# A long convolution at half-odd frequencies, over even and odd tokens, with its tables split in DRAM

## The chip, the cores and the metric

The kernel runs on one core of one Trainium2 chip. The metric is the device time of that core in microseconds, the median of several runs.

## The reference

The network has two blocks of two layers each, on 512 tokens of 1024 features. The change lies in the second block, in the long convolution of each layer (256 channels), whose kernel `k` is itself computed from the weights:

```python
    h_fwd = filt[:, :HY_WIDTH] * window
    h_bwd = filt[:, HY_WIDTH:] * window
    k = jnp.concatenate([h_fwd, jnp.zeros((1, HY_WIDTH), f32), h_bwd[:0:-1]], axis=0)
    return k * lax.rsqrt(jnp.sum(jnp.square(k), axis=0, keepdims=True) + 1e-6)
...
    k = hyena_filters(L, fw1, fb1, freq1, fw2, fb2, freq2, fw3)
    vf = jnp.fft.rfft(v, n=2 * L, axis=1)
    kf = jnp.fft.rfft(k, axis=0)
    y = jnp.fft.irfft(vf * kf[None], n=2 * L, axis=1)[:, :L]
    y = y + v * bias_d.astype(jnp.float32)
    return (y * x0.astype(jnp.float32)).astype(u.dtype)
```

With L = 512 this is a linear convolution of 512 tokens with taps at -511 to 511, by a transform of length 1024.

## The kernel before

**Products.** Every large product runs in three parts, so that it keeps the accuracy of float32: both factors are split into a high and a low part of type float32r, and `mm3` (line 347) issues high x high, high x low and low x high for each block of 128 rows. Weights come by a DMA from the SP queue into a staging buffer (`stage`, line 273); `split` (line 293) takes the high part on ACT (line 299) and the low part on DVE (line 300) into a pair of buffers of 1024 columns each, `hi` and `lo`. `pair` (line 278) hands out the pairs in turn: 3 are always there, and `more` adds some for a stretch; there are 6 in the feed-forward block of layer 1, and 3 in the part of the second block that holds the convolution. The buffers of a pair are free again when PE has read them for the last time. Staging buffers go round in the same way, 2 of them in the convolution. PSUM has 2 buffers `ps` of 512 columns that all products share, beside those that a stage opens for itself.

**Order.** Dependences and semaphores are set by the Tile framework from the order of the program. It also sets the order of the instructions on each engine: an instruction whose inputs and buffers are there earlier can stand ahead of one that comes earlier in the program. In the queue of an engine that order is then fixed, and an instruction that waits holds up what stands behind it. Streams that run beside the main one (`side`) give their steps at fixed amounts of work of the main stream.

**Spectra.** `spectrum` (line 1717) computes the transform of `k` for both layers of the second block. It runs as a side stream of the feed-forward block of layer 1, whose products are the main stream. After the filter network and the window (`sd`, sum and difference of both halves of the taps, split), it loads the table `fwd` in four parts of 256 columns (`ft`, a buffer of its own, one buffer), splits each, and multiplies: real parts with the sums, imaginary parts with the differences (two blocks of 128 frequencies in each part, 4 blocks of 128 tokens, 3 matmuls each). DVE multiplies the result with the norm `r` on its way to `K` (line 1790). A further product of 8 matmuls (line 1797) gives the highest frequency, which is packed in place of the imaginary part of frequency 0. `K` goes to DRAM (line 1801) and is loaded again by each layer's `Front` (line 1820).

**Convolution.** `second` (line 1903) runs, in the order of the program: the projections for the pooling (2 panels of 24 matmuls with 512 columns), the projections for the gate `x0` (2 such panels), beside them `values_t` (line 1858: the input of the convolution transposed, so that tokens lie on the partitions), then `transform` (line 1939), `token_values(0)` (line 1928: the first half of the attention's values, 4 blocks of tokens, 24 matmuls of 256 columns each) and `inverse` (line 1959). `attention` follows with the projections of its first head (lines 2051 to 2053).

`transform` has four blocks of 128 frequencies. For each, PE computes the real and the imaginary part in one `ps` buffer (2 x 12 matmuls of 256 columns); DVE multiplies with `K` (line 1953), POOL subtracts (line 1954), DVE adds (line 1955), and ACT and DVE split the product into `Y` (lines 360 and 361). `inverse` multiplies `Y` with the table `invt` into two `ps` buffers, one for each 128 channels (48 matmuls of 512 columns, lines 1968 to 1970); DVE, POOL, ACT and DVE finish (lines 1973 to 1975). For the tables, `transform` stages and splits four parts of `fwd`, `inverse` four parts of `invt`.

Of the kernel before, what the change touches and what calls it, by code (L numbers as in the profile page):

```python
# [18 lines left out]
S = 512  # L19
# [9 lines left out]
# ---------------------------------------------------------------------------  # L29
# host side: layout of the small vectors, tables that depend on shapes alone  # L30
# ---------------------------------------------------------------------------
# [63 lines left out]
def _constants():  # L95
# [22 lines left out]
    # attention rope: head_dim 64 = [r1 16 | r2 16 | c1 16 | c2 16], two heads on the partitions  # L118
# [12 lines left out]
    # window mask, keys [previous block | own | next]  # L131
# [4 lines left out]
    # retention rope: 64 row frequencies | 64 column frequencies  # L136
# [4 lines left out]
    # retention decay exponents  # L141
# [7 lines left out]
    # partial rope of the second block  # L149
# [11 lines left out]
    # pooling counts  # L161
# [6 lines left out]
    # hyena: position features, decay window, transform tables  # L168
# [7 lines left out]
    put("z", z)  # L176
# [4 lines left out]
    put("winf", win.reshape(4, 128, 256).transpose(1, 0, 2))  # L181
    put("winb", winb.reshape(4, 128, 256).transpose(1, 0, 2))
    con = np.ascontiguousarray(np.concatenate(out, axis=1))
    # forward [n, (cos f 0..511 | -sin f 0..511, with the Nyquist column in place of f=0)]
    fr = np.arange(512)
    ph = (2 * np.pi / 1024) * ((t[:, None].astype(np.int64) * fr[None]) % 1024)
    fwd = np.concatenate([np.cos(ph), -np.sin(ph)], axis=1)
    fwd[:, 512] = np.where(t % 2 == 0, 1.0, -1.0)
    invt = np.concatenate([2 * np.cos(ph.T), -2 * np.sin(ph.T)], axis=0) / 1024
    invt[0] = 1.0 / 1024  # L190
    invt[512] = np.where(t % 2 == 0, 1.0, -1.0) / 1024
    fwd = np.ascontiguousarray(fwd.astype(f).reshape(4, 128, 1024).transpose(1, 0, 2))
    invt = np.ascontiguousarray(invt.astype(f).reshape(8, 128, 512).transpose(1, 0, 2))
# [21 lines left out]
# ---------------------------------------------------------------------------  # L215
# device side
# ---------------------------------------------------------------------------
class Net:
# [22 lines left out]
    # -- small tables -------------------------------------------------------  # L241
# [14 lines left out]
    # -- weights ------------------------------------------------------------  # L256
# [8 lines left out]
    def stage_tile(self, some=slice(None)):  # L265
        """some: which of the rings"""
        rings = self.st_rings[some]
        n = self.si.setdefault(str(some), 0)
        pool, m = self.turn(rings, n)
        self.si[str(some)] += 1  # L270
        return pool.tile([128, 2048], F32, name=self.nm("st"), tag="st", bufs=m)
# [12 lines left out]
    def more(self, pairs, stages=0):  # L284
        """further buffers for weights"""
# [7 lines left out]
    def split(self, v):  # L293
        """f32 [128, k, c] -> hi, lo (f32r), exactly v = hi + lo up to float32's last bit"""
# [8 lines left out]
    # -- streams beside the main one, by the time of the tensor engine -------  # L303
# [13 lines left out]
    def side(self, gen, steady=False):  # L317
        """a generator whose steps each take so long; steady: on the whole, else each of them at least"""
# [12 lines left out]
    def cpanel(self, src, k, c, some=slice(None)):  # L331
        """[128, k, c] from DRAM, as pieces of 128 columns"""
# [3 lines left out]
    def kpanel(self, src, k, c):  # L336
        """[128, k, c] from DRAM, as pieces [128, 1, c]... of at most 1024 elements, listed by k"""
# [9 lines left out]
    # -- products -----------------------------------------------------------  # L347
# [15 lines left out]
    def rsqrt(self, pool, v, n):  # L363
        """[128, n] small: 1 / sqrt(v)"""
# [4 lines left out]
        # a first guess from the exponent and three steps of Newton's  # L369
# [1347 lines left out]
def spectrum(net, i, pool):  # L1717
# [61 lines left out]
    for n in range(2):  # L1779
        for j in range(2):  # L1780
# [4 lines left out]
            for jj in range(2):  # L1785
# [5 lines left out]
                if n == 0:  # L1791
                    nc.gpsimd.tensor_copy(K[:, 8 + f], K[:, f])
# [949 lines left out]
```

## Time and profile before

| | |
|---|---|
| median of 3 runs | 3169.13 us (3168.89 to 3169.70) |
| span of the profiled execution | 3174.9 us, 5.8 above that median |
| PE busy | 3008.7 us, 95% of the span |
| PE's loading of weights | 2541.3 us, 80% |
| DVE | 2021.1 us, 64% |
| ACT | 1398.8 us, 44% |
| POOL | 375.7 us, 12% |
| mean granted clock of TensorE | 0.976 of full speed |
| moved by DMA | 410.38 MB, 129 GB/s on the mean |

The profile is of one execution. Times in it are microseconds from the first instruction. PE is the tensor engine's matmul side, PEld its loading of weights, DVE the vector engine, ACT the scalar engine, POOL is GpSimd and SP the engine that issues most of the DMAs. A row names the line of the kernel, the operation, and `out<-in` by the names of the tiles. Matmuls are pipelined, so that the duration in a row is longer than the time from one to the next.

### The profile page before, as it was taken

How to read it: one execution, taken by the hardware profiler on the slowest of the kernel's cores; microseconds unless marked ns; L12 is line 12 of the kernel's file. 1: busy time of each engine (PE TensorE's matmuls, PEld its weight loads, DVE VectorE, ACT ScalarE, POOL GpSimd, SP SyncE). 2: the span in 40 equal slices, each digit the busy share in tenths (PEclk: the TensorE clock that was granted, in tenths of full speed). 3: DMA queues.
4: the chain of work that ended last, by engine and by line, in shares of the span. 5: the costliest groups of instructions: out<-in, count | busy, mean ns of one | idle time of the engine just before them, and what ended most of it. 6: DMA issues, size and time to landing. Idle time of an engine off the chain costs nothing. (4 is left out here: it accounts for less than half of the span.)

```text
span 3174.9 us, 45357 instructions
## 1 busy us (share of the span) xinstructions
PE 3008.7 (95%) x17640; PEld 2541.3 (80%) x17640; DVE 2021.1 (64%) x3944; ACT 1398.8 (44%) x2431; POOL 375.7 (12%) x362
## 2 busy tenths in 40 slices
PE   7999999999999999999999999989989989999996
PEld 4777779888888988888887788877878867788874
DVE  7688886445552754535465543668778666977865
ACT  6567773121212532323343322436555544645544
POOL 0011130000000200000010000211213211121211
PEclk8999999999999999999999999999999989999997
DMA  6112123334441222313133332231469943145994
GB/s 218 61 48 66 47 74 100 120 100 126 134 146 54 86 69 77 92 53 93 61 103 105 128 121 90 83 117 46 122 199 360 336 157 119 41 136 200 376 349 156
DMA packets 316336, 410.38 MB, mean 129 GB/s; under 512 B 15374, under 2 KB 263310, under 8 KB 314960
## 3 DMA queue, kind: packets, MB, share of 16 engines
q1 hardware_dynamic: 305744, 369.61, 35.5%
q0 software_dynamic: 10368, 37.75, 3.1%
q8 instruction: 144, 2.36, 0.3%
q14 instruction: 80, 0.66, 0.1%
HBM read 379.01 MB, written 28.31 MB: 128 GB/s over the span
## 5 line engine op out<-in xcount | busy, mean ns | idle before, releaser
L299 ACT ACTIVATE hi<-st 128x1024 fp32r<-128x1024 f32 (+1 forms) x436 | 449.7, 1035 | 637.6 <-PE ps L352 490.1
L300 DVE TENSOR_TENSOR lo<-st,hi 128x1024 fp32r<-128x1024 f32 (+1 forms) x436 | 531.6, 1222 | 197.7 <-ACT hi L299 191.8
L351 PE MATMUL ps<-hxh,hi 128*128 128x512 f32 (+1 forms) x1280 | 477.7, 374 | 5.0 <-DVE ctxT L756 2.1
L352 PE MATMUL ps<-hxl,hi 128*128 128x512 f32 (+1 forms) x1280 | 475.1, 371 | 0.3 <-DVE hxl L629 0.3
L353 PE MATMUL ps<-hxh,lo 128*128 128x512 f32 (+1 forms) x1280 | 474.4, 371 | 0.0
L351 PEld LDWEIGHTS ps<-hxh,hi 128*128 128x128 f32 x1280 | 241.9, 189 | 54.6 <-ACT sg L809 5.3
L353 PEld LDWEIGHTS ps<-hxh,lo 128*128 128x128 f32 x1280 | 242.1, 189 | 42.4 <-issue 1.2
L352 PEld LDWEIGHTS ps<-hxl,hi 128*128 128x128 f32 x1280 | 242.4, 189 | 40.8 <-issue 1.2
L351 PE MATMUL ps<-ah,hi 128*128 128x256 f32 (+1 forms) x592 | 200.7, 339 | 3.1 <-DVE x L756 1.9
L352 PE MATMUL ps<-al,hi 128*128 128x256 f32 (+1 forms) x592 | 198.7, 336 | 0.2 <-DVE al L361 0.2
L353 PE MATMUL ps<-ah,lo 128*128 128x256 f32 (+1 forms) x592 | 198.5, 335 | 0.0
L756 DVE SCALAR_TENSOR_TENSOR x<-ps,vecs,x 128x512 f32<-128x512 f32 (+1 forms) x136 | 84.4, 623 | 144.4 <-PE ps L353 144.0
L2517 PE MATMUL pa<-hi,xt 128*128 128x256 f32 x576 | 168.0, 292 | 0.6 <-ACT xt L360 0.5
L2519 PE MATMUL pa<-lo,xt 128*128 128x256 f32 x576 | 164.7, 286 | 0.0
L2518 PE MATMUL pa<-hi,xt 128*128 128x256 f32 x576 | 163.8, 284 | 0.0
L810 DVE TENSOR_TENSOR sg<-sg,ps 128x512 f32<-128x512 f32 (+1 forms) x70 | 40.0, 572 | 190.9 <-PE ps L353 190.6
L351 PEld LDWEIGHTS ps<-ah,hi 128*128 128x128 f32 x592 | 111.6, 189 | 19.7 <-DVE x L756 5.1
L351 PE MATMUL ps<-hi,hxh 128*128 128x256 f32 x416 | 120.9, 291 | 3.7 <-DVE hy L1953 1.1
L2543 PE MATMUL py<-st,at 128*128 128x512 f32 x272 | 122.7, 593 | 1.3 <-DVE y L2547 1.3
L352 PE MATMUL ps<-lo,hxh 128*128 128x256 f32 x416 | 119.8, 288 | 2.2 <-DVE lo L300 2.2
L352 PEld LDWEIGHTS ps<-al,hi 128*128 128x128 f32 x592 | 111.6, 189 | 12.5 <-DVE al L361 0.4
L353 PEld LDWEIGHTS ps<-ah,lo 128*128 128x128 f32 x592 | 111.5, 188 | 12.5
(651 smaller groups left out, 7755.3 us busy)
## 6 DMA issues: line engine op xcount, KB each, us to landing
st<-moe_w_dram SPq DMA_DIRECT2D x102, 1024.0 KB, 10.7
st<-ffn_w_in_dram SPq DMA_DIRECT2D x44, 1024.0 KB, 5.3
ast<-ada_w_dram SPq DMA_DIRECT2D x56, 512.0 KB, 4.6
st<-ret_w_qkvg_dram SPq DMA_DIRECT2D x24, 1024.0 KB, 5.2
st<-ffn_w_out_dram SPq DMA_DIRECT2D x24, 768.0 KB, 4.8
st<-ada_w_dram SPq DMA_DIRECT2D x12, 1024.0 KB, 5.2
st<-w_in_dram SPq DMA_DIRECT2D x12, 1024.0 KB, 7.5
ast<-ada_w_dram SPq DMA_DIRECT2D x8, 1024.0 KB, 12.6
```

What stands on the lines that cost most here:

```text
L299: self.nc.scalar.activation(h, v, AF.Copy)
L300: self.nc.vector.tensor_tensor(l, v, h.bitcast(F32), op=OP.subtract)
L351: self.nc.tensor.matmul(ps, wh, xh, start=(i == 0), stop=False)
L352: self.nc.tensor.matmul(ps, wh, xl, start=False, stop=False)
L353: self.nc.tensor.matmul(ps, wl, xh, start=False, stop=(i == n - 1))
L756: net.nc.vector.scalar_tensor_tensor(xm, p, self.gate[:, m:m + 1], xm, op0=OP.mult, op1=OP.add)
L810: nc.vector.tensor_tensor(sg, sg, pu, op=OP.mult)
L2517: nc.tensor.matmul(o, th[:, k], wh[:, kk], start=(k == 0), stop=False)
L2518: nc.tensor.matmul(o, tl[:, k], wh[:, kk], start=False, stop=False)
L2519: nc.tensor.matmul(o, th[:, k], wl[:, kk], start=False, stop=(k == 7))
L2543: nc.tensor.matmul(py[:, n * 512:n * 512 + 512], at[:, f], w2[f][:, 0, n * 512:n * 512 + 512], start=(f == 0), stop=(f == 1))
```

## The change

The transform is taken at the 512 frequencies f + 1/2 of a length of 1024 instead of at the 513 frequencies f. At these the real and the imaginary part fill all columns, and there is no highest frequency to pack elsewhere. The tokens are put in the order even ones, then odd ones (`eo`). For the frequencies f + 1/2 and 511 - f + 1/2 the sums over the even tokens agree but for sign and conjugation, and so do those over the odd tokens. So the products are taken for 256 frequencies only, over even and over odd tokens apart, and both sets of 256 spectra are the sum and the difference of the two. The inverse does the same the other way round. The table has half the entries; it is stored on the host as a high and a low part, in the order in which it is used. `table` loads both parts by two DMAs from POOL's queue straight into a pair, with no staging and no split.

In `spectrum`, each table serves 2 x 2 products of 6 matmuls, DVE makes sum and difference. In `transform`, PE writes PSUM buffers of its own (4 of them); ACT copies the even sums, DVE forms sum and difference, multiplies with `K`, POOL subtracts, DVE adds and forms the sum and the difference of the products for the inverse, then comes the split into `Y`. The buffers `v` and `y` are there once. In `inverse`, both tables are asked for at its start; channels go outermost, then even and odd tokens, so that 48 matmuls have 256 columns each.

```diff
@@ Net @@
+    def table(self, name, j):
+        out = []
+        for r, t in enumerate(self.pair()):
+            self.nc.gpsimd.dma_start(t, self.ins[name][:, j, r])
+            out.append(t.rearrange("p (t n c) -> p t n c", t=4, n=2) if name == "fwd" else t.rearrange("p (f c) -> p f c", f=2))
+        return out
...
@@ spectrum @@
-    for n in range(2):
-        for j in range(2):
-            c0 = n * 512 + j * 256
-            ft = pool.tile([128, 4, 256], F32, name=net.nm("ft"), tag="ft")
-            nc.sync.dma_start(ft, net.ins["fwd"][:, :, c0:c0 + 256])
-            wh, wl = net.split(ft)
-            for jj in range(2):
-                sl = slice(jj * 128, (jj + 1) * 128)
-                p = net.ps()[:, :256]
-                net.mm3(p, [(wh[:, t, sl], wl[:, t, sl], sd[n][0][:, t], sd[n][1][:, t]) for t in range(4)])
...
+    for f in range(2):
+        wh, wl = net.table("fwd", f)
+        for n in range(2):
+            ps = net.ps().rearrange("p (o c) -> p o c", o=2)
+            for o in range(2):
+                net.mm3(ps[:, o], [(wh[:, t, n], wl[:, t, n], sd[n][0][:, t], sd[n][1][:, t]) for t in (2 * o, 2 * o + 1)])
+            eo = pool.tile([128, 2, 256], F32, name=net.nm("keo"), tag="keo")
+            nc.vector.tensor_tensor(eo, ps, r[:, None, :].to_broadcast([128, 2, 256]), op=OP.mult)
+            nc.vector.tensor_tensor(Kv[:, 0, n, f], eo[:, 0], eo[:, 1], op=OP.add)
+            nc.vector.tensor_tensor(Kv[:, 1, n, f], eo[:, 0], eo[:, 1], op=OP.subtract)
+            if n == 0:
+                nc.gpsimd.tensor_copy(Kv[:, :, 2, f], Kv[:, :, 0, f])
+            yield 1.3
...
@@ values_t @@
+        vv = self.vv.rearrange("p m (n o) -> p m o n", o=2)
...
-                net.nc.tensor.transpose(p[:, m * 128:(m + 1) * 128], self.vv[:, m, t * 128:(t + 1) * 128], net.ident)
+                net.nc.tensor.transpose(p[:, m * 128:(m + 1) * 128], vv[:, m, t // 2, t % 2 * 128:t % 2 * 128 + 128], net.ident)
...
@@ transform @@
-        for j in range(2):
-            wa = net.split(net.stage(net.ins["fwd"][:, :, j * 256:j * 256 + 256], 4, 256))
-            wb = net.split(net.stage(net.ins["fwd"][:, :, 512 + j * 256:768 + j * 256], 4, 256))
...
+        for f in range(2):
+            wh, wl = net.table("fwd", f)
+            ps = [sp.tile([128, 2, 256], F32, name=net.nm("hyv"), tag="hyv", bufs=4) for _ in range(2)]
+            for o in range(2):
                 for n in range(2):
+                    net.mm3(ps[o][:, n], [(wh[:, t, n], wl[:, t, n], vt[0][:, t], vt[1][:, t]) for t in (2 * o, 2 * o + 1)])
+            v = pool.tile([128, 2, 2, 256], F32, name=net.nm("hv"), tag="hv")
+            y = pool.tile([128, 2, 4, 256], F32, name=net.nm("hy"), tag="hy")
+            nc.scalar.activation(v[:, 1], ps[0], AF.Copy)
+            nc.vector.tensor_tensor(v[:, 0], v[:, 1], ps[1], op=OP.add)
+            nc.vector.tensor_tensor(v[:, 1], v[:, 1], ps[1], op=OP.subtract)
+            for n in range(2):
+                nc.vector.tensor_tensor(y[:, :, 2 * n:2 * n + 2], v, K[:, :, n:n + 2, f], op=OP.mult)
+            nc.gpsimd.tensor_tensor(y[:, :, 0], y[:, :, 0], y[:, :, 1], op=OP.subtract)
+            nc.vector.tensor_tensor(y[:, :, 1], y[:, :, 2], y[:, :, 3], op=OP.add)
+            for o, op in enumerate((OP.add, OP.subtract)):
+                nc.vector.tensor_tensor(y[:, o, 2:4], y[:, 0, 0:2], y[:, 1, 0:2], op=op)
+            net.hilo(Y[0][:, :, :, f], Y[1][:, :, :, f], y[:, :, 2:4])
...
@@ inverse @@
-        for j in range(2):
-            pieces = net.kpanel(net.ins["invt"][:, 4 * j:4 * j + 4], 4, 512)
-            for f in range(4):
...
+        tables = [net.table("invt", j) for j in range(2)]
+        for m in range(2):
+            for o in range(2):
+                p = po[m][:, o * 256:o * 256 + 256]
+                for j, (ih, il) in enumerate(tables):
+                    for f in range(2):
+                        yh, yl = (y[:, o, j, f, m * 128:(m + 1) * 128] for y in Y)
+                        th, tl = (t[:, f, o * 256:o * 256 + 256] for t in (ih, il))
+                        nc.tensor.matmul(p, yh, th, start=(j + f == 0), stop=False)
+                        nc.tensor.matmul(p, yl, th, start=False, stop=False)
+                        nc.tensor.matmul(p, yh, tl, start=False, stop=(j + f == 2))
...
-            nc.vector.scalar_tensor_tensor(vv[:, m], vv[:, m], hb[:, m:m + 1], po[m], op0=OP.mult, op1=OP.add)
+            v2 = vv[:, m].rearrange("p (n o) -> p n o", o=2)
+            nc.vector.scalar_tensor_tensor(v2, v2, hb[:, m:m + 1], po[m].rearrange("p (o n) -> p n o", o=2), op0=OP.mult, op1=OP.add)
```

## Rows read from the trace of the kernel before

**Rows 1.** the page's busy times, shares of the span and instructions

```profile
PE 3008.7 (95%) x17640; PEld 2541.3 (80%) x17640; DVE 2021.1 (64%) x3944; ACT 1398.8 (44%) x2431; POOL 375.7 (12%) x362
```

**Rows 2.** busy time by stretch; then granted clock, DMA share, GB/s

```profile
1700.00:1880.00 180.00, 176.22 (x843) 142.76 (x842) 87.23 (x128) 59.38 (x75) 5.13 (x8) 1.00 0.36 119
...
2079.40:2093.20 13.80, 12.47 (x98) 11.76 (x96) 11.97 (x18) 5.82 (x8) 2.02 (x3) 1.00 0.58 190
2093.20:2106.30 13.10, 12.06 (x97) 11.68 (x97) 7.64 (x13) 4.76 (x8) 0.94 (x2) 1.00 0.25 81
2106.30:2118.90 12.60, 11.46 (x50) 8.79 (x48) 7.19 (x8) 4.51 (x5) 0.03 (x1) 1.00 0.44 126
2138.30:2141.70 3.40, 0.39 (x3) 0.01 (x1) 2.24 (x4) 1.29 (x3) 1.30 (x1) 1.00 0.00 0
2143.10:2146.50 3.40, 3.40 (x9) 2.65 (x9) 1.63 (x4) 1.68 (x4) 0.00 (x0) 0.51 0.45 134
```

**Rows 3.** groups of 1700 to 1880, shapes apart; busy, mean ns | idle before

```profile
L351 PE MATMUL ps<-sd,hi 128*128 128x256 f32 x64 | 18.2, 284 | 1.8 <-DVE K L1790 1.8
...
L1797 PE MATMUL ps<-sd,hi 128*128 128x256 f32 x16 | 2.2, 282 | 0.0
```

**Rows 4.** timeline of PE: start, duration, engine, line, count, idle before

```profile
2079.46 0.68 PE L351 MATMUL ps<-hvth,hi 128*128 128x256 f32 x1
2079.98 0.28 PE L352 MATMUL ps<-hvtl,hi 128*128 128x256 f32 x1
2080.10 0.28 PE L353 MATMUL ps<-hvth,lo 128*128 128x256 f32 x1
...
2084.22 0.36 PE L351 MATMUL ps<-hvth,hi 128*128 128x256 f32 x1 [1.33 <-DVE hx L1833]
...
2106.34 0.39 PE L1968 MATMUL ps<-hi,hYh 128*128 128x512 f32 x1
2106.57 0.39 PE L1969 MATMUL ps<-hi,hYl 128*128 128x512 f32 x1
...
2118.93 0.47 PE L2051 MATMUL ps<-hxh,hi 128*128 128x512 f32 x1 [1.17 <-DVE hvv L1973]
```

**Rows 5.** timeline of ACT

```profile
2067.56 1.06 ACT L299 ACTIVATE hi<-st 128x1024 fp32r<-128x1024 f32 x1 [6.24 <-PE ps L352]
...
2073.29 1.06 ACT L299 ACTIVATE hi<-st 128x1024 fp32r<-128x1024 f32 x1 [3.39 <-PE ps L352]
...
2078.98 1.06 ACT L299 ACTIVATE hi<-st 128x1024 fp32r<-128x1024 f32 x1 [3.69 <-PE ps L352]
...
2092.49 1.04 ACT L299 ACTIVATE hi<-st 128x1024 fp32r<-128x1024 f32 x1
...
2094.68 0.61 ACT L360 ACTIVATE hYh<-hy 128x512 fp32r<-128x512 f32 x1
```

**Rows 6.** timeline of POOL

```profile
2073.76 1.29 POOL L1890 TENSOR_TENSOR pu<-pu 128x512 f32<-128x512 f32 x1
```

**Rows 7.** the tile hy: ns least, median, most

```profile
L1953 DVE TENSOR_TENSOR hy<-ps,hK x16: 673/680/685, 2084.0 to 2647.9; 128x512 f32<-128x512 f32 x16
L1954 POOL TENSOR_TENSOR hy<-hy x8: 727/742/747, 2084.7 to 2648.1; 128x256 f32<-128x256 f32 x8
```

**Rows 8.** timeline of DVE

```profile
2086.95 1.23 DVE L300 TENSOR_TENSOR lo<-st,hi 128x1024 fp32r<-128x1024 f32 x1 [1.00 <-ACT hi L299]
```

**Rows 9.** the tile xg, then the tensor invt: the gathers, and times to landing

```profile
L2464 POOL DMA_INDIRECT xg<-hdram,idx x36: 935/1911/1930, 2350.8 to 3107.5; - x36
...
DMA to landing us min/median/max: 4.2/8.1/9.5
...
DMA to landing us min/median/max: 5.2/5.3/5.4
```

**Rows 10.** the tile hi, 1700 to 1880: what idle engines waited for

```profile
  PE ps L352: 64.9, 23
```

**Rows 11.** the tile hyps

```profile
L1864 PEld LDWEIGHTS hyps<-kident,hvv x16: 138/138/143, 2058.5 to 2626.7; 128*128 128x128 f32 x16
```

More of the change, by code (lines that the diff above doesn't have):

```diff
@@ L175, in _constants @@
     z[17:33] = -np.sin(wpos[None] * bands[:, None])
-    put("z", z)
+    eo = np.concatenate([t[0::2], t[1::2]])
+    put("z", z[:, eo])
     deltas = np.linspace(math.log(1e-2) / 1.5, math.log(1e-2) / 0.3, 256, dtype=f)
@@ L180, in _constants, with two @@
     winb[0] = 0.0
-    put("winf", win.reshape(4, 128, 256).transpose(1, 0, 2))
-    put("winb", winb.reshape(4, 128, 256).transpose(1, 0, 2))
+    put("winf", win[eo].reshape(4, 128, 256).transpose(1, 0, 2))
+    put("winb", winb[eo].reshape(4, 128, 256).transpose(1, 0, 2))
     con = np.ascontiguousarray(np.concatenate(out, axis=1))
[L185 to L193, printed above, removed]
+    fr = np.arange(256)
+    ph = (np.pi / 1024) * ((eo[:, None].astype(np.int64) * (2 * fr[None] + 1)) % 2048)
+    def two(m):
+        m = np.ascontiguousarray(m.astype(f))
+        hi = ((m.view(np.uint32) + np.uint32(0x800)) & np.uint32(0xFFFFF000)).view(f)
+        return np.stack([hi, m - hi], axis=1)
+    m = np.stack([np.cos(ph), -np.sin(ph)], axis=1).reshape(4, 128, 2, 2, 128).transpose(1, 3, 0, 2, 4)
+    fwd = np.stack([two(m[:, j].reshape(128, 1024)) for j in range(2)], axis=1)
+    m = np.stack([np.cos(ph.T), -np.sin(ph.T)], axis=0).reshape(2, 2, 128, 512) / 512
+    invt = np.stack([two(m[j].transpose(1, 0, 2).reshape(128, 1024)) for j in range(2)], axis=1)
+    fwd, invt = np.ascontiguousarray(fwd), np.ascontiguousarray(invt)
     return con, fwd, invt
@@ L1778, in spectrum @@
     yield 5.0
[L1779 to L1800 removed]
+    Kv = K.rearrange("p (s a f) c -> p s a f c", s=2, a=3)
+    for f in range(2):
[11 more added lines that the diff above has]
+            yield 1.3
     nc.sync.dma_start(net.kernels[i], K)
@@ L1920, in second @@
             net.finish(vt)
-            Y = [hz.tile([128, 2, 4, 256], F32R, name=net.nm("hY" + r)) for r in "hl"]
-            self.transform(Y, hz)
+            Y = [hz.tile([128, 2, 2, 2, 256], F32R, name=net.nm("hY" + r)) for r in "hl"]
+            self.transform(Y, hz, sp)
             net.finish(done[-1])
@@ L1937, in token_values @@
             yield 2.6
-    def transform(self, Y, pool):
-        net, nc, K, vt = self.net, self.net.nc, self.K, self.vt
-        for j in range(2):
-            wa = net.split(net.stage(net.ins["fwd"][:, :, j * 256:j * 256 + 256], 4, 256))
-            wb = net.split(net.stage(net.ins["fwd"][:, :, 512 + j * 256:768 + j * 256], 4, 256))
-            for jj in range(2):
-                f = 2 * j + jj
-                sl = slice(jj * 128, (jj + 1) * 128)
-                ps = net.ps().rearrange("p (a c) -> p a c", a=2)
-                for n, (wh, wl) in enumerate((wa, wb)):
-                    net.mm3(ps[:, n], [(wh[:, t, sl], wl[:, t, sl], vt[0][:, t], vt[1][:, t]) for t in range(4)])
-                y = pool.tile([128, 4, 256], F32, name=net.nm("hy"), tag="hy", bufs=2)
-                for n in range(2):
-                    k = K.rearrange("p (a f) c -> p a f c", a=3)[:, n:n + 2, f]
-                    nc.vector.tensor_tensor(y[:, 2 * n:2 * n + 2], ps, k, op=OP.mult)
-                nc.gpsimd.tensor_tensor(y[:, 0], y[:, 0], y[:, 1], op=OP.subtract)
-                nc.vector.tensor_tensor(y[:, 1], y[:, 2], y[:, 3], op=OP.add)
-                net.hilo(Y[0][:, :, f], Y[1][:, :, f], y[:, 0:2])
```

20 lines of the change are left out of this document (3 added, 17 removed).

## The prediction

> **What bounds the kernel now.** I read the page's busy shares first: TensorE works through 95% of the span, the next engine (DVE) through 64% [rows 1]. Then the table by stage, because an average hides what bounds a stage: in the feed-forward block of the second layer, where the spectra of the long convolution run as a side stream, PE is busy 176.2 of 180 us at a granted clock of 1.00 (the upper of the two levels, 2.4 GHz); in the three stages of the convolution itself (transform, values of the attention, inverse) 12.5 of 13.8, 12.1 of 13.1 and 11.5 of 12.6 us [rows 2]. So time is columns on PE, unless a wait takes their place. The timeline of PE gives the price of a column: matmuls of 256 columns follow each other after 0.12 us (0.118 in the long run), matmuls of 512 after 0.23 [rows 4]. A matmul with half the columns thus costs half; the weight load in front of it does not show.
>
> The changed stretch of a layer begins with the transform's first matmul at 2079.46 and ends where the attention's first projection starts, at 2118.93: 39.5 us [rows 4]. Of these 96 x 0.118 = 11.3 are the transform, 96 x 0.118 = 11.3 the values, 48 x 0.227 = 10.9 the inverse, 5.9 are gaps, 1.2 of them the last wait for DVE. The other layer's stretch has the same instructions, and I count it alike.
>
> **The change, part by part.** Its sum is made against the profiled execution: span 3174.9, 5.8 above the median of the runs shown, 3169.13; I take the saving over to the median as it is.
>
> *Spectra.* Before, 3 x 64 + 16 = 208 matmuls of 256 columns for both layers ([rows 3]; of the three rows of 64, one for each line of the triple, one stands); after, 2 x 48 = 96. 112 x 0.118 = 13.2 us, all on PE, which is the bound there. The 16 of the Nyquist column and its DVE work go. PE idles 1.8 us in front of these groups, for the multiplication on DVE [rows 3]; I let half of it go: **14.1 us**, bounds 13.2 and 15.0.
>
> *Table loads.* A table is now two DMAs of 512 KB issued by POOL, straight into a pair of weight buffers, instead of an early load into a staging buffer and then 1.06 us on ACT and 1.23 on DVE. It is half the table in two parts, so the bytes are the same. No row shows a plain load from POOL. The nearest are the gathers, 512 KB in the same rows of 4 KB: 0.94 to 1.93 us on POOL, 4.2 to 9.5 from issue to landing, the long ones beside the experts' weights [rows 9]; and the staged loads of 1 MB, 5.3 us [rows 9]. From the release of the pair to both halves there: 1.2 + 4.2 = 5.4 at the least, 1.9 + 9.5 = 11.4 at the most; I take 1.2 + 5.3 = **6.5**, near the quiet end, since DMA is 25 to 58% busy here [rows 2].
> The Trainium skill (DMA: Bandwidth & Descriptors, "SWDGE vs HWDGE vs iDMA") says that a float32r destination counts as a cast, which only GpSimd's software path does; by the fit of its section "Anatomy of one DMA" (2.0 us plus bytes over 436 GB/s) a half lands after an estimated 3.2 us, a table after 4.4. No run here shows it; by it the sum below would gain up to 2 us more per layer.
>
> In the feed-forward block 6 pairs go round; ACT waits for PE to free one, 64.9 us in 23 waits [rows 10], so the ring is always full, and five pairs of up to 24 matmuls (5.4 us each) lie between release and use. That hides 6.5 us; without that cover, four tables cost 26.
>
> *Convolution: PE's line.* 3 pairs go round. The pair that the first table takes is free at 2067.5, when ACT's wait for PE ends, the second's at 2073.2, the next at 2079.0 [rows 5]. POOL has additions for the pooling until 2075.05 [rows 6]; the first table is there by 2074, the second by 2081.6. The transform now takes 48 x 0.118 = 5.7 us plus the 0.4 gap behind its first matmul: first half done at 2082.7, second at 2085.6, as its four PSUM buffers of its own end the wait for DVE in its middle, now 1.33 [rows 4]. The matmuls of the values keep their 11.3; I leave them 1 us of the gaps they have (13.1 in all now): done at 2097.9.
>
> *Convolution: the vector chain.* Rows of now: a multiplication or addition of 512 elements 0.68, POOL's subtraction of 256 elements 0.74 [rows 7]; one of 512 elements on POOL 1.29 [rows 6] (with DVE beside it up to 1.8); of 1024 on DVE 1.23 [rows 8]. DVE has other work until 2084.0, when the first multiplication starts [rows 7]. First half: add, subtract, two multiplications of 1024 (3.7, beside the second POOL's subtraction), add, two sums (1.9), hi on ACT 1.06, lo on DVE 1.23: done at 2092.4. The second half waits for it, for its buffers are single: two multiplications 2.4, POOL 0.5 beyond them, 1.9, 1.1, 1.2: 2099.6; with the values' own 2.5 us on DVE up to 2102. Everything but this hides behind the values' matmuls until 2097.9.
>
> *The last table.* The inverse takes two tables. The first one's pair is free at 2085.6, and its load is hidden. The second takes the pair with the first half of the values' weights, which PE lets go 12 matmuls before their end, at 2096.5: there at **2103.0**. Six matmuls of the inverse go ahead of it, 42 x 0.118 = 5.0 follow: 2108.0. The projection starts at 2108.2, as the first of the two PSUM buffers is read while PE is on the second, and the wait of 1.2 goes. 2118.9 - 2108.2 = **10.7 us** per layer. What is queued behind the waiting table on POOL is the product with x0, which follows the inverse anyway.
>
> *Clock.* After PE has sat idle for 3.4 us, the trace shows 3.4 us at 0.51, the lower level; the nine matmuls in them would take 2.1 [rows 2], 1.3 lost. The idle time that I expect (4.4 us) is as long; I count half: 0.7. So **10.0** per layer. Weights read with a step of two in the 16 transposes cost between 0 and 1.1 us (their loads take 0.14 [rows 11]); the read of PSUM in another order, 0.7 us twice, lies beside the projection. Both stay in the range.
>
> **Sum:** 14.1 + 2 x 10.0 = 34.1; span 3140.8, time **3135**.
>
> **Rivals.**
> 1. *Nothing waits*: table and chain are ready when the values end. 2079.5 + 0.4 + 5.7 + 11.3 + 1.0 + 5.7 = 2103.6, 15.3 per layer: 3124. For it: a load at the low bound lands at 2101.9, and the order on each engine is not that of the program (ACT takes a later split, 2092.49, ahead of a hi, 2094.68 [rows 5]), so a buffer may come free sooner. Against it: the chain alone ends at 2099.6 or later.
> 2. *A table queued behind POOL's own work.* POOL runs in order. If the second table is issued behind the first half's subtraction, it lands at 2088 + 6.5 = 2094.5 where PE wants it at 2082.7; the values end at 2109.7, the last table lands at 2114.8, the projection starts at 2119.9: the convolution gains nothing, 3155. A landing at 11.4 us for each table, served one after another, comes to the same. For it: in the program the table stands behind that subtraction. Against it: the staged loads of now are issued as soon as a buffer is free.
> 3. *Slower: the load from POOL takes far longer than the gathers.* With T from release to both halves landed, the three exposed loads put the projection at 2085.1 + 3T; gain over all 14.1 + 2 x (33.8 - 3T) = 81.7 - 6T. It turns at T = 13.6; at 16 the time is 3183. The rows reach 11.4 under heavy traffic. The Trainium skill (SBUF — State Buffer, "Who interferes with whom") has a way to it: descriptors for a load from GpSimd wait while DVE runs a copy or tensor_scalar in a 2-port mode. The rows of DVE here are tensor_tensor and reads of PSUM but for few, so the trace gives it little room.
> 4. *The feed-forward block doesn't hide its tables:* 3135 + 26 = 3161.
> 5. *The halved work is not the bound:* if the splits of the values' weights are queued behind both halves of the chain, PE starts the values at 2102.3, ends them at 2114.6, gets the last table at 2119.7 and the projection starts at 2124.7: 5.8 lost per layer, 3167. Against it: today's order takes those splits early [rows 5].
>
> **How the numbers follow.** Forecast 0.52 (own range 3127 to 3143), rival 1 0.14, rival 2 0.17, rival 3 0.08, rival 4 0.04, rival 5 0.05. The range runs from 3121, below rival 1, to 3158, above rival 2. Faster by over 0.2% (6.3 us, about what a measurement of this kernel can tell): 0.52 + 0.14 + 0.17 + 0.04 = 0.87; within 0.2% rival 5, 0.05; slower 0.08.
>
> **What would show it.** In the profile after: 96 matmuls of the spectra, with no waits for a DMA among them; PE idle some 4 us in front of the inverse's seventh matmul, with the second inverse table's landing named as releaser (or DVE's lo, if the chain is last); from the transform's first matmul to the projection 28 to 29 us. A wait between the transform's halves means rival 2 or 3: POOL's timeline tells which, by whether the issue or the landing is late. A table over 13 us after its pair is free, or a gap in the feed-forward block in front of a table's first matmul, makes the prediction wrong.

## The result, and the profile after

| | before | after |
|---|---|---|
| median of 4 runs each, us | 3169.4 (3168.9 to 3172.4) | 3139.7 (3134.7 to 3142.7) |
| ratio | | 0.9902, 95% interval 0.9888 to 0.9916 |
| span of the profiled execution | 3174.9 | 3138.5 (its own time 3140.3) |
| TensorE busy, matmuls | 3008.7 us, 17640 | 2976.7 us, 17432 |

The change is faster by 29.7 us; 34.1 were forecast. The two spans differ by more, 36.4, because the profiled execution of before was long: its span alone is above the time of each run in the table. So I compare stretches with a common start below, and medians for the whole.

The page's busy times of after, with the rows that answer to [rows 1]:

```profile
PE 2976.7 (95%) x17432; PEld 2513.2 (80%) x17432; DVE 2005.7 (64%) x3924; ACT 1377.3 (44%) x2407; POOL 386.2 (12%) x378
```

The same stretches of after as in [rows 2]: the spectra's feed-forward block, then transform, values and inverse of layer 0, and within the inverse the part at the lower clock (PE, PEld, DVE, ACT, POOL busy; granted clock; DMA share; GB/s):

```profile
1700.00:1880.00 180.00, 178.04 (x797) 142.83 (x796) 89.18 (x131) 57.15 (x74) 4.61 (x8) 0.99 0.39 127
2063.60:2069.70 6.10, 6.10 (x50) 5.86 (x49) 5.45 (x7) 3.50 (x5) 0.00 (x0) 1.00 0.00 0
2069.70:2081.70 12.00, 11.73 (x98) 11.53 (x97) 10.97 (x15) 2.94 (x6) 4.56 (x4) 1.00 0.42 132
2081.70:2094.40 12.70, 9.21 (x49) 8.51 (x50) 5.34 (x8) 2.50 (x4) 3.16 (x4) 0.73 0.42 125
2085.60:2092.40 6.80, 5.97 (x26) 5.68 (x27) 2.06 (x3) 0.06 (x1) 0.00 (x0) 0.50 0.53 169
```

Transform and values run without a gap, the transform in 6.1 us where before took 13.8. The inverse has half the columns of before and takes as long as before (12.7 against 12.6 us): PE idles in it, and then works at half the clock. PE's timeline of after shows what it waits for there (start, duration, engine, line, out<-in, shape, count, idle before and its releaser):

```profile
2063.60 0.68 PE L368 MATMUL hyv<-hvth,hi 128*128 128x256 f32 x1
...
2081.15 0.28 PE L370 MATMUL ps<-hi,hxl 128*128 128x256 f32 x1
2081.76 0.39 PE L1984 MATMUL ps<-hi,hYh 128*128 128x256 f32 x1 [0.33 <-DVE dvl L378]
...
2084.95 0.38 PE L1984 MATMUL ps<-hi,hYh 128*128 128x256 f32 x1 [2.58 <-DVE dvl L378]
...
2087.22 0.58 PE L1985 MATMUL ps<-hi,hYl 128*128 128x256 f32 x1 [0.71 <-DVE hYl L378]
...
2088.68 0.41 PE L1985 MATMUL ps<-hi,hYl 128*128 128x256 f32 x1
...
2094.38 0.40 PE L2068 MATMUL ps<-hxh,hi 128*128 128x512 f32 x1
```

Three waits for DVE, none for a DMA. The first two are for PSUM buffers: the inverse adds up in the two buffers through which the values pass, and the eviction of the last values (dvl) stands in DVE's queue behind the products. The third is for the last step of the vector chain (hYl). DVE's timeline of the same stretch:

```profile
2079.01 2.36 DVE L1966 TENSOR_TENSOR hy<-hv,hK 128x1024 f32<-128x1024 f32 x2
2081.29 0.42 DVE L378 TENSOR_TENSOR dvl<-ps,dvh 128x256 fp32r<-128x256 f32 x1
2082.54 0.69 DVE L1968 TENSOR_TENSOR hy<-hy 128x512 f32<-128x512 f32 x1 [0.84 <-POOL hy L1967]
2083.27 1.29 DVE L1970 TENSOR_TENSOR hy<-hy 128x512 f32<-128x512 f32 x2
2084.48 0.42 DVE L378 TENSOR_TENSOR dvl<-ps,dvh 128x256 fp32r<-128x256 f32 x1
2084.82 1.22 DVE L309 TENSOR_TENSOR lo<-st,hi 128x1024 fp32r<-128x1024 f32 x1
2085.95 1.22 DVE L378 TENSOR_TENSOR hYl<-hy,hYh 128x1024 fp32r<-128x1024 f32 x1
```

The chain ends at 2087.17, 23.6 us behind the transform's first matmul. Ahead of its last step stands a split of the attention's weights (L309). POOL's timeline, and the landing of the second inverse table's halves (issues of 2082 to 2084: KB, us from issue to landing):

```profile
2080.40 2.11 POOL L1967 TENSOR_TENSOR hy<-hy 128x512 f32<-128x512 f32 x1 [6.31 <-DVE hy L1966]
2082.46 0.57 POOL L360 DMA_DIRECT2D hi<-invt_dram  x1
2083.03 0.54 POOL L360 DMA_DIRECT2D lo<-invt_dram  x1
...
hi<-invt_dram POOLq DMA_DIRECT2D x1, 512.0 KB, 4.3
lo<-invt_dram POOLq DMA_DIRECT2D x1, 512.0 KB, 5.0
```

The low half is there at 2083.03 + 5.0 = 2088.0, 24.4 us behind the start: the table and the chain come almost together, and which of them costs the time is not to be read from this profile. Behind the inverse POOL waits for a load. This wait is in before too (POOL's timeline of before, then of after):

```profile
2129.19 1.29 POOL L2060 TENSOR_TENSOR df<-df,krc 128x512 f32<-128x512 f32 x1 [7.76 <-DMA krc<-con_dram]
...
2106.32 1.29 POOL L2077 TENSOR_TENSOR df<-df,krc 128x512 f32<-128x512 f32 x1 [7.95 <-DMA krc<-con_dram]
```

The attention's rope tables (krc) take memory that the convolution holds to its end. Counted from the attention's first projection, this row starts later in after: 11.9 us and 12.4 in the two layers, against 10.3 and 8.6 in before.

### The profile page after: what moved, and what is told of

Same layout as the page of the kernel before. It is cut to its first block, busy times and chain, and to the rows that moved or that the text cites. A ratio compares the mean times of both kernels' runs of the same rounds, so it can differ in the third digit from the quotient of the medians.

```text
span 3138.5 us, 44857 instructions
## 1 busy us (share of the span) xinstructions
PE 2976.7 (95%) x17432; PEld 2513.2 (80%) x17432; DVE 2005.7 (64%) x3924; ACT 1377.3 (44%) x2407; POOL 386.2 (12%) x378
## 5 line engine op out<-in xcount | busy, mean ns | idle before, releaser
L308 ACT ACTIVATE hi<-st 128x1024 fp32r<-128x1024 f32 (+1 forms) x420 | 433.7, 1035 | 644.6 <-PE ps L369 503.7
L309 DVE TENSOR_TENSOR lo<-st,hi 128x1024 fp32r<-128x1024 f32 (+1 forms) x420 | 512.2, 1222 | 182.0 <-ACT hi L308 177.5
L604 POOL TENSOR_TENSOR nacc<-nacc,nsq 128x256 f32<-128x256 f32 x56 | 51.1, 912 | 599.4 <-ACT nsq L603 597.8
L369 PEld LDWEIGHTS ps<-al,hi 128*128 128x128 f32 x592 | 111.6, 188 | 12.4 <-DVE al L378 0.4
```

The costliest lines, as they stand in the source:

```text
L308: self.nc.scalar.activation(h, v, AF.Copy)
L309: self.nc.vector.tensor_tensor(l, v, h.bitcast(F32), op=OP.subtract)
L369: self.nc.tensor.matmul(ps, wh, xl, start=False, stop=False)
L604: nc.gpsimd.tensor_tensor(self.acc, self.acc, sq, op=OP.add)
```

## The experiments

I read two kinds of marks off PE's timeline. For the spectra: from the first matmul of their filter to the last of layer 0's first projections (wl), where the work between is the same but for the spectra. In before and after:

```profile
1632.72 0.64 PE L1746 MATMUL ps<-zt,fw 33*64 33x512 f32 x1
...
2053.56 0.28 PE L353 MATMUL wl<-hxh,lo 128*128 128x256 f32 x1
```

```profile
1630.06 0.64 PE L1763 MATMUL ps<-zt,fw 33*64 33x512 f32 x1
...
2037.78 0.28 PE L370 MATMUL wl<-hxh,lo 128*128 128x256 f32 x1
```

420.8 against 407.7 us. For the convolution: from that last wl matmul to the output of the inverse (the attention's first projection), to the first scores and to the last scores, as a mean over the two layers. Kernels with the same instructions there show how far such a mark holds: before and spectra_only differ by 0.4, 1.2 and 1.9 us, after and conv_only by 0.2, 1.4 and 2.0.

| kernel | median us | ratio to before, 95% interval | spectra's mark | projection | first scores | last scores |
|---|---|---|---|---|---|---|
| before | 3169.4 | 1 | 420.8 | 65.5 | 87.4 | 190.9 |
| after | 3139.7 | 0.9902 (0.9888 to 0.9916) | 407.7 | 56.7 | 80.6 | 182.4 |
| spectra_only | 3151.7 | 0.9953 (0.9936 to 0.9970) | 407.6 | 65.1 | 86.2 | 189.0 |
| conv_only | 3155.1 | 0.9953 (0.9938 to 0.9969) | 420.7 | 56.9 | 82.0 | 184.4 |
| split_on_chip | 3141.0 | 0.9918 (0.9902 to 0.9933) | 409.4 | 58.8 | 82.2 | 184.0 |
| own_last_table | 3145.6 | 0.9917 (0.9902 to 0.9931) | 408.7 | 58.2 | 79.8 | 182.7 |
| sub_on_dve | 3137.6 | 0.9896 (0.9878 to 0.9913) | 407.4 | 55.8 | 80.1 | 181.4 |
| both_moved | 3142.8 | 0.9905 (0.9885 to 0.9925) | 407.4 | 57.3 | 79.4 | 181.7 |
| filled_idle | 3139.7 | 0.9897 (0.9880 to 0.9915) | 408.0 | 55.6 | 78.8 | 180.7 |
| rope_early | 3136.7 | 0.9898 (0.9882 to 0.9915) | 407.3 | 56.2 | 76.2 | 179.7 |
| x0_behind | 3130.2 | 0.9881 (0.9865 to 0.9898) | 407.6 | 52.6 | 74.3 | 177.3 |
| x0_behind_rope | 3131.3 | 0.9877 (0.9860 to 0.9893) | 409.2 | 52.5 | 72.4 | 175.9 |
| x0_behind_counts | 3129.0 | 0.9871 (0.9854 to 0.9889) | 406.1 | 51.1 | 72.5 | 176.1 |
| x0_behind_counts_rope | 3127.2 | 0.9859 (0.9841 to 0.9876) | 407.4 | 52.2 | 72.4 | 175.3 |

In each group the kernel before ran beside them (medians 3168.1, 3171.3, 3169.3 and 3171.1), and the ratio goes by those runs.

### Where the gain lies

**spectra_only** has the convolution of before, with tables for the new frequencies:

```
-            wh, wl = net.table("fwd", f)
-            ps = [sp.tile([128, 2, 256], F32, ...) for _ in range(2)]
+            wa = net.split(net.stage(net.ins["fwdf"][:, :, j * 256:j * 256 + 256], 4, 256))
...
```

> The spectra of the change with the convolution of the kernel before (its 512 frequencies as one table of all tokens, staged by SP and split on the chip; the same frequencies f + 1/2, so the computation is whole). The theory, that the two halves of the change gain in separate places, expects the spectra's part alone: between 14.1 us, the matmul columns that go by full-clock rows of before, and 15.9 us, by which the first transform came earlier in the profile after: 3153.5 to 3155.5 us against 3169.4. The rival, that the spectra's matmuls were not what the wide FFN waits for, so that all of the gain is the convolution's, expects 3167 to 3171.

**conv_only** has the spectra of before instead:

```
-    for f in range(2):
-        wh, wl = net.table("fwd", f)
...
+    for n in range(2):
+        for j in range(2):
...
+            nc.sync.dma_start(ft, net.ins["fwdf"][:, :, c0:c0 + 256])
+            wh, wl = net.split(ft)
...
```

The product for the highest frequency runs here too, and its result is not used.

> The convolution of the change (half tables split in DRAM, sums and differences) with spectra that are computed as before, by 192 + 16 matmuls over one table of all tokens, at the frequencies f + 1/2. The theory of separate gains expects the change's whole 29.7 us less the 14 to 16 of the spectra: 13.8 to 15.6, or 6.9 to 7.8 a layer: 3154 to 3155.5 us. By the profiles' own milestones, 5.7 to 8.8 a layer at the first scores and the output projection, it is 3152 to 3158. If the convolution stands alone behind the result, 3139 to 3142.

Both ratios are 0.9953, about 15 us each, and the two savings together are the change's. The spectra's mark is sharper: 13.1 us less in the kernels with the new spectra than in those with the old, which is 112 matmuls at 0.118 (13.2). The convolution is 8.2 to 8.8 us a layer shorter at the projection, and 4.2 to 6.8 at the first scores, by the two pairs of kernels: part of it is given back at the attention's start.

**split_on_chip** asks what the split in DRAM is worth:

```
-            self.nc.gpsimd.dma_start(t, self.ins[name][:, j, r])
...
+        self.nc.sync.dma_start(v, self.ins[name][:, j].rearrange("p (k c) -> p k c", k=4))
+        return [... for t in self.split(v)]
```

> All of the change but the tables' split: the same half tables come whole from DRAM by SP's queue through stage tiles, and ACT and DVE split them, 1.06 and 1.23 us for each of four a layer. The theory that the halved matmuls carry the gain expects the spectra's part to stay, since wide FFN work hides the splits, and the convolution to give back up to one DVE and one ACT split of each inverse table in its chain and the wait for stage tiles: 1 to 5 us a layer, 3142 to 3150 us. The rival, that the table split in DRAM is what pays, expects most of the gain gone: 3155 us and more. If the split lies beside other work everywhere: 3138 to 3142.

The convolution loses 2.1 us a layer at the projection and 1.6 at the first scores, the latter hardly more than the mark's error; the spectra's mark is within 2 us. So nearly all of the gain is the halved matmuls. By these marks the split in DRAM brings 3 to 4 of the 30 us, at the low end of the first expectation; the median, 3141.0, lies in the range of the third, and the ratios can't tell the two kernels apart. Where it costs is on DVE (timelines of DVE and PE of split_on_chip):

```profile
2068.84 2.32 DVE L308 TENSOR_TENSOR lo<-st,hi 128x1024 fp32r<-128x1024 f32 x1
...
2074.56 0.39 PE L369 MATMUL ps<-hi,hxh 128*128 128x256 f32 x1 [2.82 <-DVE dvl L379]
```

This split of a table, 1.22 us elsewhere, takes 2.32 beside POOL's subtraction. The values' evictions wait behind it, and PE waits 2.82 us for one of them inside the values.

### What ends last in front of the inverse

**own_last_table:**

```
+            if f:
+                own = {j: net.table("invt", j, [pool.tile([128, 1024], F32R, ...) for r in "hl"]) for j in (1,)}
...
-        tables = [net.table("invt", j) for j in range(2)]
+        tables = [own[j] if j in own else net.table("invt", j) for j in range(2)]
```

> The change with buffers of its own for the second inverse table, so that its load waits for no weight pair and is issued ahead of POOL's subtractions. The theory that the vector chain and this table tie (in the profile after the chain ends 23.6 us after the first transform matmul, the table's low half lands at 24.5) expects that PE then waits for the chain alone: 0.5 to 1.5 us a layer, 3136.5 to 3139 us against 3139.7; in the trace the second inverse table lands before the token values end, and PE still waits for hYl. The rival, that the table alone holds the inverse, expects the inverse to run without a wait after its first matmuls: 3 us a layer and more, 3134 us or less. A third, that the earlier load only competes with the panels of w_in that SP loads at that time, expects 3140 and more.

**sub_on_dve:**

```
-            nc.gpsimd.tensor_tensor(y[:, :, 0], y[:, :, 0], y[:, :, 1], op=OP.subtract)
+            nc.vector.tensor_tensor(y[:, :, 0], y[:, :, 0], y[:, :, 1], op=OP.subtract)
```

> The change with the products' subtraction on DVE (0.69 us for the addition of the same shape there) in place of POOL (2.11 to 2.21 us). The theory of the tie expects both ends to come earlier: the chain by 1.4 to 2.2 us a layer, and the second inverse table's issue by up to 2.7, since POOL has nothing in front of it: 3135 to 3137 us. The rival, that DVE's queue is the chain (it runs the evictions of the token values and the splits of weights between the chain's steps), expects no difference: 3138 to 3141.

**both_moved** has both edits:

> Both of the edits together: own buffers for the second inverse table, and the subtraction on DVE. If chain and table tie, this gives more than either alone: the chain ends about 21.5 us after the first transform matmul, some 3 us of idle time and part of the half-clock stretch go: 2 to 4 us a layer, 3132 to 3136 us. If the chain alone sets the end, it equals the kernel with the subtraction on DVE within 1 us; if the table alone does, it equals the kernel with the table's own buffers.

**filled_idle:**

```
             run(self.token_values(0))
+            idle = sp.tile([128, S], F32, ...)[:, :256]
+            for d in range(40):
+                nc.tensor.matmul(idle, self.vt[d % 2][:, d % 4, :128], self.vt[0][:, d % 4], start=True, stop=True)
```

> The change with 40 further matmuls of 256 columns (4.7 us at 0.118 each) between the token values and the inverse, into a PSUM tile that nobody reads: PE is busy where it idled, and nothing else is altered. The theory that the idle stretch costs a second time, by the half clock of the inverse's matmuls after it (PEclk 0.73 over 12.7 us in the profile after), expects the clock to stay at 1.00 and 2 to 3 us a layer back: 3134 to 3136 us. The rival, that the inverse's matmuls were long because their operands came late, expects nothing back, or the loss of what the further matmuls run past the chain's end: 3139 to 3142.

None of the four differs from after in its total by more than its interval (the runs of both_moved alone go from 3134.1 to 3151.0). The stretch itself speaks more plainly. In us behind the transform's first matmul, layer 0 / layer 1, with the chain's end (the end of the last hYl on DVE):

| kernel | chain ends | projection starts | between |
|---|---|---|---|
| after | 23.6 / 23.6 | 30.8 / 30.2 | 7.2 / 6.7 |
| own_last_table | 24.6 / 24.6 | 32.0 / 31.9 | 7.4 / 7.3 |
| sub_on_dve | 22.8 / 22.8 | 29.1 / 29.9 | 6.3 / 7.1 |
| both_moved | 23.9 / 23.9 | 31.4 / 30.7 | 7.5 / 6.8 |
| filled_idle | 23.6 / 23.6 | 29.5 / 29.3 | 5.9 / 5.7 |

The chain's end is the same in both layers to 0.03 us. What comes behind it is not: conv_only and rope_early, with the instructions of after in this stretch, also end the chain at 23.6, and start the projection at 29.8 to 31.0.

The table was not the limit: with its own buffers it is issued at 2031 in layer 0, and the projection starts later, not earlier. The chain ends later there as well, but in both_moved it ends only 0.3 us later than in after, with the table there long before, and the projection is no earlier either. The tie falls, and my expectation with it. So does the third reading, competition with the panels: the transform starts 25.9 and 26.6 us behind the last wl matmul, in after 25.8 and 26.6. What the edit does instead is in DVE's timeline of own_last_table:

```profile
2083.27 1.22 DVE L309 TENSOR_TENSOR lo<-st,hi 128x1024 fp32r<-128x1024 f32 x1
2084.41 1.28 DVE L1972 TENSOR_TENSOR hy<-hy 128x512 f32<-128x512 f32 x2
2085.61 0.41 DVE L378 TENSOR_TENSOR dvl<-ps,dvh 128x256 fp32r<-128x256 f32 x1
2085.94 1.21 DVE L309 TENSOR_TENSOR lo<-st,hi 128x1024 fp32r<-128x1024 f32 x1
2087.08 1.22 DVE L378 TENSOR_TENSOR hYl<-hy,hYh 128x1024 fp32r<-128x1024 f32 x1
```

The weight pair that the table no longer takes goes to a panel of the attention, and one more split comes into DVE's queue between the chain's steps: 2 x 1.2 us ahead of hYl, where after has one. The table's hold on that pair had kept the split away. With the subtraction on DVE the chain ends 0.7 us earlier in both layers (1.4 to 2.2 were expected). The projection follows by 1.7 in layer 0 and by 0.3 in layer 1: the granted clock over the inverse is 0.84 in that layer 0, and 0.71 to 0.76 in layer 1 and in both layers of the other kernels of the table but filled_idle. With both edits, two splits are ahead of hYl again and the gain is gone. So the chain, as DVE's queue orders it, ends last, and its end moves by what stands between its steps. The Trainium skill (SBUF — State Buffer, "Who interferes with whom") says that a DVE instruction with two inputs in SBUF contends with a GpSimd instruction that reads SBUF. The rows agree: POOL's subtraction takes 2.11 us beside the second product, the same shape 1.29 alone [rows 6].

filled_idle shows the clock's share (stretches of the further matmuls and of the inverse):

```profile
2083.70:2088.50 4.80, 4.80 (x42) 4.80 (x41) 3.90 (x8) 2.39 (x3) 2.30 (x3) 1.00 0.46 118
2088.50:2095.50 7.00, 6.18 (x50) 5.78 (x49) 1.85 (x2) 0.47 (x1) 1.29 (x1) 1.00 0.46 146
```

The clock stays at 1.00, and the inverse's matmuls are busy for 6.2 us where after has 9.2. From the chain's end to the projection it is 5.9 and 5.7 us, where the six layers with the same instructions (two each of after, conv_only and rope_early) take 6.2 to 7.4: the half clock costs 1.1 us a layer on the mean (0.4 to 1.6), not the 3.0 by which the busy time falls. The slow matmuls ahead of the chain's end would have waited anyway, and at the full clock PE comes to the second inverse table before its low half is there (PE's timeline of filled_idle):

```profile
2090.68 0.39 PE L1989 MATMUL ps<-lo,hYh 128*128 128x256 f32 x1 [0.28 <-DMA lo<-invt_dram]
```

That half lands 24.6 us behind the start and holds this matmul up by 0.4 us in layer 0, so the table lies right behind the chain. I had expected 2 to 3 us a layer, and by its median, 3139.7, the kernel lies in the rival's range.

### What is given back, and a faster kernel

**rope_early:**

```
+        self.rope = net.con(vp, "rc2"), net.con(vp, "rs2")
...
-    rc, rs = net.con(pool, "rc2"), net.con(pool, "rs2")
+    rc, rs = rope
```

> The change with the attention's two rope tables loaded at the start of the second stage, into the pool of the values, and not when the convolution's memory comes free. In the profile after POOL waits 7.95 us and DVE 2.94 us for them, and PE idles 2.56 us in layer 0 and 3.06 and 1.84 us in layer 1 before the first scores. The theory that these tables now come last there, and give back part of the convolution's gain, expects the first scores 2 to 4 us earlier behind the first transform matmul (54.4 us in the profile after): 3132 to 3136 us against 3139.7. The rival, that the chain of the first head (eviction, shuffle, rope, the splits of q and k on ACT and DVE) is as late without them, expects 0 to 1 us a layer: 3138 to 3141.

The first scores come 4.4 us a layer earlier, the last scores 2.7; the median falls by 3.1 us, to 3136.7, just outside the expected 3132 to 3136, and the intervals overlap. PE still idles at the first scores, now for the head's splits on ACT (PE's timeline of rope_early):

```profile
2113.42 0.50 PE L2104 MATMUL dsc<-dkh,dq 128*128 128x512 f32 x1 [2.68 <-ACT dkh L2092]
```

**x0_behind** puts useful work where PE idled (with own_last_table's edit, not shown again):

```
-            for m, w in enumerate(net.cpanel(win[:, :, 0:256], 8, 256)):
-                p = net.ps()
-                self.proj(p, w)
+            st = net.stage(win[:, :, 0:256], 8, 256)
+            def x0(m, p):
+                self.proj(p, net.split(st[:, :, m * 128:m * 128 + 128]))
                 self.conv(m, self.x0[:, m], p)
+            x0(0, net.ps())
...
             run(self.token_values(0))
+            for m in (1,):
+                x0(m, sp.tile([128, S], F32, ..., tag="hyps", bufs=2))
```

> The change with the second x0 projection (24 matmuls of 512 columns, 5.1 us) moved from before the transform to between the token values and the inverse, where PE idles, and with buffers of its own for the second inverse table. PE then has 22.9 us of work behind the first transform matmul, against a vector chain that ends 22.8 to 24.6 us behind it by the profiles so far. The theory that idle time and half clock in this stretch cost some 7 us a layer expects 3 to 6 us a layer back: 3128 to 3134 us, with PEclk above 0.9 in the inverse. The rivals: the transform, 5.1 us earlier, waits for its fourth block of turned tokens (in the profile after it was there only 2.4 us before the first matmul) and the time only moves to its front, 3136 to 3140; or the projection's split and two evictions (some 3.5 us on DVE) come into DVE's queue ahead of the chain's end, and the inverse starts as late as before, 3138 to 3142.

**x0_behind_rope** adds the rope tables' early load:

> Both: the second x0 projection behind the token values, and the rope tables loaded at the start of the second stage. The two stretches follow each other on PE, so the theories expect the sum of the two kernels' gains: 3120 to 3130 us. If what the first gives is lost at the attention's start, or the rope tables' earlier load (0.5 MB on SP's queue) delays the pooling's and the projections' loads, it is no faster than the better of the two alone.

x0_behind takes 4.1 us a layer off at the projection and 5.0 at the last scores: the idle stretch and the clock do cost what was thought, and 3130.2 us lies within the expectation. The rival is there too, in part: in layer 0 the transform waits 2.3 us in its first half for its last turned block, which in DVE's queue stands behind the pooling's late counts (DVE's timeline of x0_behind):

```profile
2055.11 1.41 DVE L1904 TENSOR_TENSOR pic<-pu,pic 64x512 f32<-64x512 f32 x2 [4.41 <-DMA pic<-con_dram]
2056.55 0.69 DVE L1905 TENSOR_TENSOR pic<-pic,pu 128x512 f32<-128x512 f32 x1
2057.16 0.42 DVE L378 TENSOR_TENSOR hvtl<-hyps,hvth 128x256 fp32r<-128x256 f32 x1
```

The rope tables add nothing that the time shows: 1.9 us at the first scores and 1.4 at the last, about the marks' error. My sum of the two was wrong. In x0_behind POOL's product with the tables already starts 9.2 and 8.6 us behind the projection, about as in before (10.3 and 8.6), so less was left for them to bring.

**x0_behind_counts** gives those counts two buffers, and **x0_behind_counts_rope** has all of it:

```
-        ic = pool.tile([128, S], F32, name=net.nm("pic"), tag="pic")
+        ic = pool.tile([128, S], F32, name=net.nm("pic"), tag="pic", bufs=2)
```

> The kernel with the second x0 projection behind the token values, and two buffers for the pooling's counts. In its trace before, the second pooling half waits 4.41 us on DVE for its counts, whose load waits for the first half's buffer, and behind it in DVE's queue stands the split of the fourth block of turned tokens, for which the transform then idles 2.45 us in layer 0. If that wait is what the earlier transform ran into, the idle stretch inside the transform goes and the first transform half takes about 3 us, not 5.5: 2 to 3 us a layer, 3124 to 3128 us against 3130. If the table's load or the panel's split is as late, no more than 1 us a layer: 3128 to 3132.

> The same with the rope tables loaded at the start of the second stage as well. The rope tables alone brought the first scores 3.9 to 5.0 us earlier, of which 1.8 to 3.6 were left at the last scores. If that holds here, 3 to 6 us less than without: 3119 to 3125 us. If the attention's later heads give it back (its vector work, not its start, sets its length), within 2 us of the kernel without them.

The wait inside the transform is gone (0.3 us left), and the projection comes 1.5 us earlier; the median falls by 1.2, the lesser of the two expectations. Rope tables on top: 1.8 us less by the medians, so the second theory. Together it is 0.9859 of before (0.9841 to 0.9876), 3127.2 us: the fastest kernel here by the median, and below the change's whole interval; the intervals of the four kernels with x0 behind overlap. The inverse of all four waits 1.1 to 1.9 us for the first inverse table, which still takes a pair of the ring (PE's timeline of x0_behind_counts_rope), so something is left:

```profile
2084.15 0.36 PE L1994 MATMUL ps<-hi,hYh 128*128 128x256 f32 x1 [1.85 <-DMA hi<-invt_dram]
```

## Why the prediction held, point by point

**Spectra: right.** 13.1 us by the mark against 14.1; the 0.9 for half of the gaps did not come, the lower bound 13.2 did. No matmul of the block waits for a table, as the **feed-forward cover** had it.

**Table loads: right in size.** The halves take 4.2 to 6.9 us from issue to landing and 0.53 to 0.80 on POOL to issue. The last table was there 5.6 us behind its issue (2082.46 to 2088.0). The 6.5 were counted from the pair's release, and from there it is about 7.9: POOL issues the table 18.9 us behind the start, in sub_on_dve, with no subtraction on POOL ahead of it, at 16.6. The Trainium skill's fit for this path (DMA: Bandwidth & Descriptors, "Anatomy of one DMA"), an estimated 3.2 us for a half, is below the shortest row.

**PE's line: right.** The transform takes 6.1 us as worked out; the values end 17.7 us after the start, forecast 18.4.

**The vector chain: the mis-sized term.** Forecast 20.1 to 22.5 us behind the start, measured 23.6, and it decides (own_last_table, both_moved). Two prices were low. POOL's subtraction was put at 0.5 us beyond the products; the next step starts 1.2 behind them (2081.37 to 2082.54), in both halves. And the queue's other work was counted at 2.5 us, where a split of the attention's weights, 1.2 us, also stands ahead of the last step. The PSUM buffers, which wait for the values' last eviction in that same queue, I had not seen at all.

**The last table: the wrong one of two.** It lands at 24.4 us, forecast 23.5; as the step that sets the end it was wrong, since taking its wait away brings no earlier projection. The prediction's last paragraph names DVE's lo as the other possibility. That the idle time up to the chain's end came out right (4.8 us with 0.118 for each matmul in it, forecast 4.4) is luck: the chain ends at 23.6 us, where the table was forecast.

**Clock:** 0.7 a layer forecast; 1.1 on the mean by filled_idle, 0.4 to 1.6.

**Sum.** 10.7 less 0.7 a layer was forecast for the convolution, 8.2 to 8.8 are there at the projection. The last step in front of the inverse came when it was forecast (23.6 against 23.5 us), so the difference lies behind it: from there to the projection 5.2 and 0.7 for the clock were forecast, and 6.2 to 7.4 are measured in the six layers, 6.9 on the mean. And before's other layer, counted alike, takes 39.0 us, not 39.5. After that the forecast ended, and there it missed what is **given back**: 2 to 4 us a layer by the first scores, where the rope tables come later than in before. Loaded early they bring 4.4 back there, more than was given back, since before waits for them too. At the last scores the two pairs of kernels leave 4.6 to 8.6 a layer; with the spectra's 13.1 that is 22.3 to 30.3, which holds the 29.7.

**The rivals.** That nothing waits (3124) fell by PE's waits. The table behind POOL's own work is what POOL's timeline shows for the second inverse table, issued right behind the subtraction, but it cost nothing by itself; for the second transform table it did not happen. A slow load, an uncovered feed-forward block and halved work off the bound are ruled out by the landings, the spectra's mark and the values, which follow the transform without a gap.

## What to carry to other kernels

Halving the columns of a bound engine gives what the columns say where other work stands beside it (13.1 of 13.2 us), and less where a chain on another engine is then the longer one: there put an independent product into the gap, which brought 4.1 us a layer, where the best shortening of the chain moved its end by 0.7. Freeing a shared buffer is not free: whoever takes it next queues its own work, and here that work went ahead of the chain. And follow a saved stretch on to the next common point, since a load that waits for its memory can take back a quarter of the gain and more: here 2 to 4 us of some 8.5 a layer by the first scores.

## What the runs showed of the hardware

- POOL and DVE slow each other when both read two operands from SBUF: 2.11 to 2.21 us against 1.29 on POOL, 2.32 against 1.22 on DVE. DVE's two products beside the subtraction keep their time, 2.36 us for both. Work moved to POOL to relieve DVE buys less than its own time says.
- A float32r load of 512 KB from POOL's queue takes 0.53 to 0.80 us of POOL's time and 4.2 to 6.9 us to land in after (3.9 to 9.2 over all kernels here).
- PE idles 2.9 of the 4.4 us from 2081.2 to 2085.6, and then shows 6.8 us at 0.50, the lower of its two levels (1.2 GHz); kept at work over the same stretch it stays at 1.00. With the same instructions the stretch at 0.50 lasts 3.4 us in layer 0 of rope_early (2087.15 to 2090.55) and 6.8 in the five other layers of after, conv_only and rope_early, so a single execution tells the price of the clock only to about 1 us.
- The stretch ahead of the changed work differs by up to 6 us between executions of kernels with equal instructions there (2053.56 in before and 2047.55 in conv_only for the same matmul), so marks from a common start are needed to see 1 us.
